# Strassen's seven products for the down projection of a two-layer decoder trunk

## The chip, the cores and the metric

The kernel runs on one core of one Trainium2 chip. The metric is the device time of one launch in microseconds. The core has TensorE (PE: matmuls; PEld: its weight loads), VectorE (DVE), ScalarE (ACT), GpSimd (POOL) and SyncE (SP, which issues DMAs here). Each takes its instructions in order and waits on semaphores for the others.

## The reference

Two layers of a hybrid decoder block over 256 tokens of 1024 features, all in float32. The first half of a layer (attention, a recurrent branch, a pooling branch, gates, an output projection) is not touched. The second half is the MLP:

```python
m = rms_norm(h, norm_mlp_pre[l])
y = jnp.square(jax.nn.relu(m @ w_mlp_up[l])) @ w_mlp_down[l]
h = h + rms_norm(y, norm_mlp_post[l])
```

Here m is 256 x 1024, w_mlp_up is 1024 x 4096 and w_mlp_down is 4096 x 1024.

## The kernel before

**Precision.** Each float32 operand is split into a high part, rounded to the fast format fp32r by ACT (`A.activation(hi, src, AF.Copy)`, L84), and a low part, the rest, by DVE (`V.tensor_tensor(... op=ALU.subtract)`, L85). A product is then three matmuls into the same PSUM bank: high by high, high by low, low by high (`mm3`, L91 to L94). So every weight that is used passes once through ACT and once through DVE.

**Weights.** They lie in memory as tiles of 128 x 1024 in the order of use. `load_to` (L130) issues a DMA on SP into one of four raw buffers (`NRAW`); `split_to` (L138) makes the pair `wh`, `wl` in one of eight buffers each; `take` hands out the next pairs in order, and `ahead` (L159) splits two tiles in advance. A raw buffer is free again when its last reader is done, and the DMA of a later tile waits for that.

**The MLP.** The 4096 hidden features are done in eight chunks of 512. `up` (L725) makes one chunk: for each of its two units of 256 features `w_unit` (L276) issues 48 matmuls of 256 columns into one bank, ACT takes the ReLU and the square, and the result is split into `hid`. The first chunk (`up_first`, L698) is made with tokens as rows and is turned by PE transposes (`hidden_T`). `down` (L737) adds one chunk's part of the result into four PSUM banks `yb` (two halves of tokens by two halves of output columns) that stay open over all chunks: for each 256 hidden features 24 matmuls of 512 columns (`s_hu`, L289). The order on PE is up of chunk f, then down of chunk f - 1. The last two chunks are done token half by token half, so that the norm of the first half (`residual`, L253) runs beside the matmuls of the second.

**What sets the order.** A scheduler in the tile framework puts each engine's instructions in order from the program's order, priorities and its own estimate of durations, and gives each new tile of a pool the buffer that it expects to be free first. The order is fixed when the program is built.

Of the kernel before, what the change touches and what calls it, by code (L numbers as in the profile page):

```python
# [16 lines left out]
L = 2  # L17
D = 1024
# [14 lines left out]
AHEAD = 2  # L33
RGD = 4
FINE = (8, 8)
SQRT_2_PI = 0.7978845608028654


# [13 lines left out]

def trunk(ctx, tc, x, wts, rgw, par, gpost, eye, ctab, out):
    nc = tc.nc
    V, A, PE = nc.vector, nc.scalar, nc.tensor

    const = ctx.enter_context(tc.tile_pool(name="const", bufs=1))
    raws = ctx.enter_context(tc.tile_pool(name="raws", bufs=NRAW))
# [14 lines left out]
    def ttile(shape, dt=F32, nm="t"):  # L73
        return tmp.tile(shape, dt, tag="t", name=nm)
# [4 lines left out]
    def bank(shape, nm="ps"):  # L79
        return psum.tile(shape, F32, tag="b", name=nm)  # L80

    def split(hi, lo, src, scale=None):
        if scale is None:
            A.activation(hi, src, AF.Copy)  # L84
            V.tensor_tensor(out=lo, in0=src, in1=hi.bitcast(F32), op=ALU.subtract)  # L85
        else:
            A.activation(hi, src, AF.Copy, scale=scale)
            V.scalar_tensor_tensor(out=lo, in0=src, scalar=scale, in1=hi.bitcast(F32),
                                   op0=ALU.mult, op1=ALU.subtract)
# [244 lines left out]
    for l in range(L):  # L334
# [355 lines left out]

        gB = gpool.tile([P, D], F32, tag="g", name="gB2")
        nc.sync.dma_start(gB[:], gpost[l, 1])
        yb = [[bank([P, 512]) for _ in range(2)] for _ in range(2)]

        def new_hidden():
            return (acts.tile([P, 2, 4, T], F32R, tag="hi", name="hid"))

        def up_first():  # L698
            hus = take(4)
            hid = new_hidden()  # L700
            zs = []

            def hidden_T(tt):
                p2 = bank([P, 4, P])
                for j in range(4):
                    PE.transpose(p2[:, j, :], zs[tt][:, j * P:(j + 1) * P], ident)
                split(hid[:, 0, :, tt * P:(tt + 1) * P], hid[:, 1, :, tt * P:(tt + 1) * P], p2[:])

            for tt in range(2):
                ps = bank([P, 512])  # L710
                for u in range(2):
                    w = [[t_.rearrange("p (k n) -> p k n", k=4)[:, k, :] for hu in hus[2 * u:2 * u + 2]
                          for k in range(4) for t_ in hu[i:i + 1]] for i in range(2)]
                    by_pass(ps[:, u * 256:(u + 1) * 256], uh, ul, w[0], w[1], tt,
                            mid=(lambda: mlp_in(1)) if tt == 0 and u == 1 else None)
                z = ttile([P, 512], nm="z")
                A.activation(z[:], ps[:], AF.Relu)
                V.tensor_tensor(out=z[:], in0=z[:], in1=z[:], op=ALU.mult)
                zs.append(z)
            later(1, lambda: hidden_T(0))  # L720
            later(1, lambda: hidden_T(1))
            ahead()
            return hid

        def up(fc):  # L725
            hid = new_hidden()
            for u in range(2):
                ps = w_unit(take(2), uh, ul)
                tick()
                z = ttile([P, 2, T], nm="z")  # L730
                A.activation(z[:], ps[:], AF.Relu)
                A.activation(z[:], z[:], AF.Square)
                split(hid[:, 0, 2 * u:2 * u + 2, :], hid[:, 1, 2 * u:2 * u + 2, :], z[:])
                ahead()
            return hid

        def down(fc, hid):  # L737
            for nh in range(2):
                for i in range(2):
                    hu, = take(1)  # L740
                    for tt in range(2):
                        s_hu(yb[tt][nh][:], hu, hid[:, 0], hid[:, 1], 2 * i, tt, fc == 0 and i == 0, False)
                    ahead()

        hid = up_first()
        for fc in range(1, 7):
            nxt = up(fc)
            down(fc - 1, hid)
            hid = nxt
        hids = [hid, up(7)]  # L750
        hus = take(8)
        un = []
        if l + 1 < L:
            uh, ul = new_pair("u")
        for tt in range(2):
            for f in range(2):
                for nh in range(2):
                    for i in range(2):
                        if tt == 1 and f == 1 and nh == 1 and i == 0 and l + 1 < L:
                            mix_features(0, un[0], l + 1)  # L760
                        s_hu(yb[tt][nh][:], hus[4 * f + 2 * nh + i], hids[f][:, 0], hids[f][:, 1], 2 * i, tt,
                             False, f == 1 and i == 1)
            residual(tt, yb[tt], msq[tt], gB)
            if l + 1 < L:
                un.append(mix_norm(tt))
            else:
                for hf in range(2):
                    sl = slice(hf * 512, (hf + 1) * 512)
                    nc.sync.dma_start(out[tt * P:(tt + 1) * P, sl], h[:, tt, sl])
# [37 lines left out]
def _layout(i):  # L807
    qc = np.concatenate([np.arange(hd * 64, hd * 64 + 64) for hd in _HEADS])
    units, rg, par, gp = [], [], [], []
    for l in range(L):  # L810
        w = i["w_in"][l]
        o = np.cumsum([0, 1024, 256, 256, 1024, 1024, 1024, 1024, 1024, 1024])
        q, kv, xr, yr, pp = w[:, :1024][:, qc], w[:, 1024:1536], w[:, o[3]:o[4]], w[:, o[4]:o[5]], w[:, o[5]:o[6]]
        ga, gr, gpl = w[:, o[6]:o[7]], w[:, o[7]:o[8]], w[:, o[8]:o[9]]
        units.append(_s_units(kv)[0])
        for u in _s_units(q):
            units.append(u)
        by = {"pg": i["w_pool_groups"][l].reshape(2, 2, 2, P, 256).transpose(0, 3, 1, 2, 4).reshape(2, 1, P, HU_COLS)}
        for nm, m in (("pp", pp), ("yr", yr), ("xr", xr)):
            by[nm] = _w_units(m).reshape(4, 2, P, HU_COLS)  # L820
        for nm, m in (("gp", gpl), ("ga", ga), ("gr", gr), ("bp", i["w_pool_br"][l]), ("ba", i["w_attn_br"][l][qc]),
                      ("br", i["w_rnn_br"][l])):
            by[nm] = _s_units(m)
        for nm in ORDER:
            units.append(by[nm[0:2]][int(nm[2])])
        for u in _s_units(i["w_out"][l]):
            units.append(u)
        up = _w_units(i["w_mlp_up"][l]).reshape(8, 4, P, HU_COLS)
        dn = _s_units(i["w_mlp_down"][l]).reshape(2, 8, 2, P, HU_COLS).transpose(1, 0, 2, 3, 4).reshape(8, 4, P, HU_COLS)
        units.append(up[0])  # L830
        for f in range(1, 8):
            units.append(up[f])
            units.append(dn[f - 1])
        units.append(dn[7])
# [34 lines left out]
```

## Time and profile before

| | us |
|---|---|
| median of 2 runs (964.25 to 965.38) | 964.82 |
| the profiled execution | 964.16 |
| its span, first to last instruction | 962.3 |
| down projection of layer 0, first matmul | 326.4 |
| last matmul of the program | 955.55 |

The granted TensorE clock is 0.999 of full speed. The rows that carry the argument stand in the prediction. To read them: a row of a timeline is start, duration, engine, line, operation, output<-inputs; the bracket is the engine's idle time just ahead and what ended it. A row of a group has the count, the busy time, the mean in ns, then the idle time before.

### The profile page before, as it was taken

Reading aid. Unit: us, or ns where it says so; the run is one execution under the profiler, and the core shown is the slowest. Engines: PE = TensorE matmul, PEld = TensorE weight load, DVE = VectorE, ACT = ScalarE, POOL = GpSimd, SP = SyncE. Lnnn points to the kernel's source line nnn. Section 1 sums busy time; section 2 is a strip of 40 time slices with the busy share of each in tenths; the row PEclk is TensorE's granted clock in tenths of the full one; section 3 lists DMA queues with packets and bytes.
Section 4 is the critical chain, followed back from the end, with each engine's and each line's share of the span. In section 5 each row is a group of like instructions: output and inputs, shape, how many; then the busy total and the mean of one; then the engine's idle time right before and its main releaser. Section 6 shows DMA issues by size and latency. Waiting matters only on the chain.

```text
span 962.3 us, 14953 instructions
## 1 busy us (share of the span) xinstructions
PE 951.3 (99%) x5716; PEld 835.3 (87%) x5716; DVE 649.7 (68%) x1101; ACT 599.8 (62%) x1001; POOL 2.6 (0%) x20
## 2 busy tenths in 40 slices
PE   8999999999999999999999999999999999999997
PEld 5898988988888999999888989888888899999995
DVE  6877886779768645445586778777897585545542
ACT  7754864789737655455566657566895476555541
POOL 0000000000000000000000000000000000000000
PEclk9999999999999999999999999999999999999999
DMA  7765456453755766665457536536358285665631
GB/s 277 244 205 185 132 166 195 161 178 111 254 161 176 226 192 192 183 192 176 134 183 257 172 111 210 179 103 219 124 178 262 88 276 179 195 185 188 185 122 44
DMA packets 48743, 173.28 MB, mean 180 GB/s; under 512 B 5408, under 2 KB 5792, under 8 KB 48672
## 3 DMA queue, kind: packets, MB, share of 16 engines
q1 hardware_dynamic: 48384, 172.16, 55.4%
q8 instruction: 45, 0.74, 0.3%
q14 instruction: 26, 0.21, 0.1%
q10 hardware_dynamic: 288, 0.17, 0.1%
HBM read 171.26 MB, written 1.05 MB: 179 GB/s over the span
## 4 chain that ended last, share of the span: by engine, by line
PE 97%; DMA 1%; ACT 1%; DVE 1%; issue 0%; SPq 0%; DVEq 0%; ACTq 0%
PE ps L92 28%; PE ps L93 28%; PE ps L94 28%; PE ps L303 8%; PE ps L391 1%; PE ps L439 1%; PE ps L428 1%; DMA raw<-wts 1%; PE ps L216 1%; PE ps L371 0%; PE ps L619 0%; ACT wh L84 0%; DVE h L269 0%; ACT junk L229 0%; DVE wl L85 0%
## 5 line engine op out<-in xcount | busy, mean ns | idle before, releaser
L85 DVE TENSOR_TENSOR wl<-raw,wh 128x1024 fp32r<-128x1024 f32 (+1 forms) x348 | 385.7, 1123 | 189.1 <-ACT wh L84 180.4
L84 ACT ACTIVATE wh<-raw 128x1024 fp32r<-128x1024 f32 (+1 forms) x348 | 334.2, 986 | 242.6 <-PE ps L94 106.2
L92 PE MATMUL ps<-mh,wh 128*128 128x256 f32 x448 | 126.9, 283 | 0.0
L94 PE MATMUL ps<-mh,wl 128*128 128x256 f32 x448 | 126.8, 283 | 0.0
L93 PE MATMUL ps<-ml,wh 128*128 128x256 f32 x448 | 126.8, 283 | 0.0
L92 PE MATMUL ps<-uh,wh 128*128 128x256 f32 x384 | 109.0, 284 | 0.0
L93 PE MATMUL ps<-ul,wh 128*128 128x256 f32 x384 | 108.7, 283 | 0.0
L94 PE MATMUL ps<-uh,wl 128*128 128x256 f32 x384 | 108.6, 283 | 0.0
L93 PE MATMUL ps<-wl,hid 128*128 128x512 f32 x256 | 99.9, 390 | 0.0
L92 PE MATMUL ps<-wh,hid 128*128 128x512 f32 x256 | 99.8, 390 | 0.0
L94 PE MATMUL ps<-wh,hid 128*128 128x512 f32 x256 | 99.6, 389 | 0.0
L92 PEld LDWEIGHTS ps<-mh,wh 128*128 128x128 f32 x448 | 86.0, 192 | 0.5
L93 PEld LDWEIGHTS ps<-ml,wh 128*128 128x128 f32 x448 | 85.9, 192 | 0.5
L94 PEld LDWEIGHTS ps<-mh,wl 128*128 128x128 f32 x448 | 86.0, 192 | 0.0
L92 PE MATMUL ps<-wh,uh 128*128 128x512 f32 x200 | 79.2, 396 | 0.7 <-ACT uh L222 0.7
L94 PE MATMUL ps<-wh,ul 128*128 128x512 f32 x200 | 78.1, 390 | 0.4 <-DVE ul L224 0.4
L93 PE MATMUL ps<-wl,uh 128*128 128x512 f32 x200 | 78.1, 390 | 0.0
L92 PEld LDWEIGHTS ps<-uh,wh 128*128 128x128 f32 x384 | 73.6, 192 | 1.1 <-issue 0.7
L93 PEld LDWEIGHTS ps<-ul,wh 128*128 128x128 f32 x384 | 73.6, 192 | 0.4
L94 PEld LDWEIGHTS ps<-uh,wl 128*128 128x128 f32 x384 | 73.6, 192 | 0.0
L94 PEld LDWEIGHTS ps<-wh,hid 128*128 128x128 f32 x256 | 48.1, 188 | 10.0
L92 PEld LDWEIGHTS ps<-wh,hid 128*128 128x128 f32 x256 | 48.1, 188 | 9.7
(190 smaller groups left out, 1589.8 us busy)
## 6 DMA issues: line engine op xcount, KB each, us to landing
raw<-wts SPq DMA_DIRECT2D x316, 512.0 KB, 4.3
gB<-gpost SPq DMA_DIRECT2D x4, 512.0 KB, 4.6
rg<-rgw SPq DMA_DIRECT2D x8, 256.0 KB, 3.9
out<-h SPq DMA_DIRECT2D x4, 256.0 KB, 2.1
h<-x SPq DMA_DIRECT2D x2, 256.0 KB, 3.3
h<-x SPq DMA_DIRECT2D x1, 512.0 KB, 7.0
cst<-ctab SPq DMA_DIRECT2D x1, 168.0 KB, 4.8
prm<-par ACTq DMA_DIRECT2D x1, 104.0 KB, 3.7
```

Of the source, the lines that this page charges most:

```text
L84: A.activation(hi, src, AF.Copy)
L85: V.tensor_tensor(out=lo, in0=src, in1=hi.bitcast(F32), op=ALU.subtract)
L92: PE.matmul(o, lh, rh, start=start, stop=False, **kw)
L93: PE.matmul(o, lh, rl, start=False, stop=False, **kw)
L94: PE.matmul(o, ll, rh, start=False, stop=stop, **kw)
L216: PE.transpose(banks[c // 4][:, c % 4, :], src[c // 4][:, (c % 4) * P:(c % 4 + 1) * P], ident)
L303: PE.matmul(o, xx[:, c, tsl], ww[c], start=(n == 0 and c == 0), stop=(n == 2 and c == 7))
L391: PE.matmul(sc[hd // hp][:, hd % hp, :], qT[a, j // 2][rows, j % 2, blk * P:(blk + 1) * P], kTs[0][rows, a, 0:w], start=True, stop=True)
L428: PE.transpose(ps[:, g, :], g8["p"](4 * b + g)[:, kt * P:(kt + 1) * P], ident)
L439: PE.matmul(ps[b * 64:b * 64 + 64, :, :], vt[kt][:, 256 + kv * 64:256 + kv * 64 + 64], g8[b, kt][:], start=(kt == 0), stop=(kt == nk - 1))
```

## The change

The down projection is done in 16 blocks (`NBLK`) of 256 hidden features. In the first 13 of layer 0 and 14 of layer 1 a block's product, 256 tokens by 256 features times 256 features by 1024 columns, is taken as a 2 x 2 block product and computed by Strassen's scheme in Winograd's form: seven products of 128 x 128 by 128 x 512, each of three matmuls, in place of eight. Each product adds into a bank of its own over all these blocks (`prods`, seven banks), and five additions at the end (`drain`) combine them. The last three and two blocks (`PLAIN`) are done as before, into the same banks.

The scheme needs four sums of weight quarters (`weight_sums`) and four of activation quarters (`hidden_forms`) per block. They are computed on POOL. Of the operands, b11 of the second weight tile (`bh`, `bl`), the first weight tile (`dh`, `dl`) and the four weight sums (`sh`, `sl`, two pairs) are split, and so are three quarters and four sums of the activations (`xf`). The host puts the weight tiles in another order and swaps the halves of every second tile of a block.

```diff
+PLAIN = (3, 2)
+NBLK = 16
...
+            for j in range(2):
+                zs[j] = ttile([P, 2, T], nm="z")
...
-                split(hid[:, 0, :, tt * P:(tt + 1) * P], hid[:, 1, :, tt * P:(tt + 1) * P], p2[:])
+                for j in range(2):
+                    A.activation(zs[j][:, :, tt * P:(tt + 1) * P], p2[:, 2 * j:2 * j + 2, :], AF.Copy)
...
+        def up(j):
+            ps = w_unit(take(2), uh, ul)
+            tick()
+            z = ttile([P, 2, T], nm="z")
+            A.activation(z[:], ps[:], AF.Relu)
+            A.activation(z[:], z[:], AF.Square)
+            zs[j] = z
+        def hidden_forms(j):
+            z = zs.pop(j)
+            a12, a22, a11, a21 = [z[:, i // 2, (i % 2) * P:(i % 2 + 1) * P] for i in range(4)]
+            sm = ttile([P, 4, P], nm="sm")
+            G.tensor_tensor(sm[:, 0, :], a21, a22, op=ALU.add)
+            G.tensor_tensor(sm[:, 2, :], a11, a21, op=ALU.subtract)
+            G.tensor_tensor(sm[:, 1, :], sm[:, 0, :], a11, op=ALU.subtract)
+            G.tensor_tensor(sm[:, 3, :], a12, sm[:, 1, :], op=ALU.subtract)
+            f = acts.tile([P, 2, 7, P], F32R, tag="hi", name="xf")
+            zf = z.rearrange("p c t -> p (c t)")[:, 0:384]
+            split(f[:, 0, 0:3, :].rearrange("p b t -> p (b t)"), f[:, 1, 0:3, :].rearrange("p b t -> p (b t)"), zf)
+            split(f[:, 0, 3:7, :], f[:, 1, 3:7, :], sm[:])
+            forms[j] = f
+        def weight_sums(j):
+            load_to(st["split"] + 2)
+            r0, r1 = raw_t.pop(st["split"]), raw_t.pop(st["split"] + 1)
...
+            b21, b22, b12, b11 = r0[:, 0:512], r0[:, 512:1024], r1[:, 0:512], r1[:, 512:1024]
+            t8 = acts.tile([P, 4, 512], F32, tag="lo", name="wsum")
+            G.tensor_tensor(t8[:, 0, :], b22, b12, op=ALU.subtract)
+            G.tensor_tensor(t8[:, 1, :], b12, b11, op=ALU.subtract)
+            G.tensor_tensor(t8[:, 2, :], b22, t8[:, 1, :], op=ALU.subtract)
+            G.tensor_tensor(t8[:, 3, :], b21, t8[:, 2, :], op=ALU.subtract)
...
+            split(w1[0][:], w1[1][:], r0[:])
+            split(w4[0][:], w4[1][:], b11)
+            wforms[j] = [w1, w4, t8]
+            load_to(st["split"] + 3)
+        def weight_forms(j):
+            t8 = wforms[j].pop()
+            for i in range(2):
...
+                split(w[0][:], w[1][:], t8[:, 2 * i:2 * i + 2, :].rearrange("p b n -> p (b n)"))
+                wforms[j].append(w)
+        def down(j):
+            f = forms.pop(j)
+            w1, w4, w2, w3 = wforms.pop(j)
+            lo_, up_ = slice(0, 512), slice(512, 1024)
+            for p, blk, w, cs in ((2, 0, w1, lo_), (1, 2, w4, lo_), (3, 6, w1, up_), (5, 3, w2, up_), (7, 5, w2, lo_),
+                                  (6, 4, w3, lo_), (4, 1, w3, up_)):
+                if p not in prods:
+                    prods[p] = bank([P, 512], nm="pr")
+                first, last = j == 0, j == nstr - 1 and p in (1, 5, 6, 7)
+                mm3(prods[p][:], f[:, 0, blk, :], f[:, 1, blk, :], w[0][:, cs], w[1][:, cs], first, last)
+        up_first()
+        split_to(st["use"] + 2)
+        up(2)
+        weight_sums(0)
+        split_to(st["use"] + 2)
+        weight_forms(0)
+        hidden_forms(0)
+        for j in range(nstr):
+            if j + 3 < NBLK:
+                up(j + 3)
+            if j + 1 < nstr:
+                weight_sums(j + 1)
+                hidden_forms(j + 1)
+            if j + 4 < NBLK:
+                split_to(st["use"] + 2)
+            down(j)
+            if j + 1 < nstr:
+                weight_forms(j + 1)
...
+            s1 = ttile([P, 512], nm="s1")
+            A.activation(s1[:], prods[1][:], AF.Copy)
+            u2, u4, u3 = [ttile([P, 512], nm="us") for _ in range(3)]
+            V.tensor_tensor(out=u2[:], in0=prods[6][:], in1=s1[:], op=ALU.add)
+            V.tensor_tensor(out=u4[:], in0=prods[5][:], in1=u2[:], op=ALU.add)
+            V.tensor_tensor(out=u3[:], in0=prods[7][:], in1=u2[:], op=ALU.add)
+            u5 = ttile([P, 512], nm="us")
+            V.tensor_tensor(out=u5[:], in0=prods[7][:], in1=u4[:], op=ALU.add)
+            return [[s1, u4], [u3, u5]]
...
+            for nh in range(2):
+                V.tensor_tensor(out=ys[nh][:], in0=tgt[tt][nh][:], in1=ys[nh][:], op=ALU.add)
+            residual(tt, ys, msq[tt], gB)
```

**How the order moves.** On PE an up projection of 48 matmuls and a block's 21 of the down projection now alternate. Three other places matter, all in the middle of layer 0's MLP.

ACT before, one chunk: `z` is the hidden chunk, `wh` the high parts of weight tiles (the number behind the name is the tile's place in memory).

```order
314 L731 ACTIVATE z_3866<-ps_3817 128x512
315 L732 ACTIVATE z_3866<-z_3866 128x512
316 L84 ACTIVATE hid_3816<-z_3866 128x512
317 L84 ACTIVATE wh124_4076<-raw124_3983 128x1024
318 L84 ACTIVATE wh125_4080<-raw125_4001 128x1024
319 L731 ACTIVATE z_3932<-ps_3883 128x512
320 L732 ACTIVATE z_3932<-z_3932 128x512
321 L84 ACTIVATE hid_3816<-z_3932 128x512
```

ACT now, a little over one block: `wh126`, `wh127` are up weights; `dh_4042`, `bh_4044`, `sh_4097`, `sh_4101` belong to the block with raw tiles 120 and 121, whose weight sums are `wsum_4037` and whose activations are `xf_4059`.

```order
333 L87 ACTIVATE sh_4097<-wsum_4037 128x1024
334 L87 ACTIVATE sh_4101<-wsum_4037 128x1024
335 L732 ACTIVATE z_4034<-ps_3985 128x512
336 L87 ACTIVATE bh_4044<-raw121_3952 128x512
337 L733 ACTIVATE z_4034<-z_4034 128x512
338 L87 ACTIVATE dh_4162<-raw124_4052 128x1024
339 L87 ACTIVATE xf_4059<-sm_4054 128x512
340 L87 ACTIVATE wh126_4184<-raw126_4074 128x1024
341 L87 ACTIVATE xf_4179<-z_3914 128x384
342 L87 ACTIVATE wh127_4188<-raw127_4170 128x1024
343 L87 ACTIVATE sh_4217<-wsum_4157 128x1024
344 L87 ACTIVATE sh_4221<-wsum_4157 128x1024
```

Ahead of the split of an up tile stands now the form of `sm` (row 339), which waits for POOL. Before, only PE and the loads were waited for there.

POOL had 8 memsets a layer and nothing in the MLP. Its rows now, with the semaphores that they wait for (DMAHW are the loads): the sums of raw tiles 124 and 125, then the activation sums of the block ahead of them, then the sums of raw tiles 128 and 129.

```order
59 L759 TENSOR_TENSOR wsum_4157<-raw124_4052,raw125_4072 128x512 [waits DMAHW1_49,DMAHW0_49,DVE_49]
60 L760 TENSOR_TENSOR wsum_4157<-raw125_4072 128x512
61 L761 TENSOR_TENSOR wsum_4157<-raw124_4052,wsum_4157 128x512 [waits Pool_49]
62 L762 TENSOR_TENSOR wsum_4157<-raw124_4052,wsum_4157 128x512 [waits Pool_49]
63 L742 TENSOR_TENSOR sm_4054<-z_3794 128x128
64 L743 TENSOR_TENSOR sm_4054<-z_3794 128x128
65 L744 TENSOR_TENSOR sm_4054<-sm_4054,z_3794 128x128 [waits Pool_49]
66 L745 TENSOR_TENSOR sm_4054<-z_3794,sm_4054 128x128 [waits Pool_49]
67 L759 TENSOR_TENSOR wsum_4277<-raw128_4172,raw129_4192 128x512 [waits DMAHW5_49,DMAHW4_49,DVE_49]
```

So `sm_4054`, of the block with raw tiles 120 and 121, is made only after the weight sums of the next block (rows 59 to 62), and those wait for that block's raw tiles.

SP, the loads, before and then now, with their waits: tiles in the order in which they are used.

```order
134 L134 DMA raw123_3965<-wts 128x1024 [waits DMAHW3_49,DVE_49]
135 L134 DMA raw124_3983<-wts 128x1024 [waits DMAHW4_49,DVE_49]
136 L134 DMA raw125_4001<-wts 128x1024 [waits DMAHW5_49,DVE_49]
137 L134 DMA raw126_4019<-wts 128x1024 [waits DMAHW6_49,DVE_49]
138 L134 DMA raw127_4084<-wts 128x1024 [waits DMAHW7_49,DVE_49]
```

```order
135 L137 DMA raw124_4052<-wts 128x1024 [waits DMAHW4_49,DVE_49,Pool_49]
136 L137 DMA raw125_4072<-wts 128x1024 [waits DMAHW6_49,DVE_49]
137 L137 DMA raw126_4074<-wts 128x1024 [waits DMAHW7_49,DVE_49]
138 L137 DMA raw127_4170<-wts 128x1024 [waits DMAHW5_49,DVE_49]
139 L137 DMA raw128_4172<-wts 128x1024 [waits DMAHW0_49,DVE_49,Pool_49]
140 L137 DMA raw129_4192<-wts 128x1024 [waits DMAHW2_49,DVE_49]
```

Before, each load waits for the DVE split of the tile that held its buffer. Now the first raw tile of every block waits for POOL (128 takes the buffer of 124, after its last sum), and the second takes the buffer of an up tile: 129 that of 126, so that it waits for the DVE half of the split of `wh126`.

More of the change, by code (lines that the diff above doesn't have):

```diff
@@ L54, in trunk @@
     nc = tc.nc
-    V, A, PE = nc.vector, nc.scalar, nc.tensor
+    V, A, PE, G = nc.vector, nc.scalar, nc.tensor, nc.gpsimd
     const = ctx.enter_context(tc.tile_pool(name="const", bufs=1))
@@ L692, in trunk @@
         nc.sync.dma_start(gB[:], gpost[l, 1])
-        yb = [[bank([P, 512]) for _ in range(2)] for _ in range(2)]
-        def new_hidden():
-            return (acts.tile([P, 2, 4, T], F32R, tag="hi", name="hid"))
+        nstr = NBLK - PLAIN[l]
+        prods = {}
+        zs, forms, wforms = {}, {}, {}
         def up_first():
             hus = take(4)
-            hid = new_hidden()
-            zs = []
+            toks = []
+            for j in range(2):
+                zs[j] = ttile([P, 2, T], nm="z")
             def hidden_T(tt):
@@ L705, in hidden_T @@
                 for j in range(4):
-                    PE.transpose(p2[:, j, :], zs[tt][:, j * P:(j + 1) * P], ident)
-                split(hid[:, 0, :, tt * P:(tt + 1) * P], hid[:, 1, :, tt * P:(tt + 1) * P], p2[:])
+                    PE.transpose(p2[:, j, :], toks[tt][:, j * P:(j + 1) * P], ident)
+                for j in range(2):
+                    A.activation(zs[j][:, :, tt * P:(tt + 1) * P], p2[:, 2 * j:2 * j + 2, :], AF.Copy)
             for tt in range(2):
@@ L715, in up_first @@
                             mid=(lambda: mlp_in(1)) if tt == 0 and u == 1 else None)
-                z = ttile([P, 512], nm="z")
+                z = ttile([P, 512], nm="zt")
                 A.activation(z[:], ps[:], AF.Relu)
                 V.tensor_tensor(out=z[:], in0=z[:], in1=z[:], op=ALU.mult)
-                zs.append(z)
+                toks.append(z)
             later(1, lambda: hidden_T(0))
             later(1, lambda: hidden_T(1))
[L722 to L751, printed above, removed]
+        def up(j):
[5 more added lines that the diff above has]
+            zs[j] = z
@@ new lines, in weight_sums @@
+        def weight_sums(j):
+            load_to(st["split"] + 2)
+            r0, r1 = raw_t.pop(st["split"]), raw_t.pop(st["split"] + 1)
+            st["split"] += 2
+            st["use"] += 2
+            b21, b22, b12, b11 = r0[:, 0:512], r0[:, 512:1024], r1[:, 0:512], r1[:, 512:1024]
[4 more added lines that the diff above has]
+            G.tensor_tensor(t8[:, 3, :], b21, t8[:, 2, :], op=ALU.subtract)
+            w1 = (his.tile([P, HU_COLS], F32R, tag="wh", name="dh"), los.tile([P, HU_COLS], F32R, tag="wl", name="dl"))
+            w4 = (ttile([P, 512], F32R, nm="bh"), ttile([P, 512], F32R, nm="bl"))
+            split(w1[0][:], w1[1][:], r0[:])
+            split(w4[0][:], w4[1][:], b11)
+            wforms[j] = [w1, w4, t8]
+            load_to(st["split"] + 3)
@@ new lines, in weight_forms @@
+        def weight_forms(j):
+            t8 = wforms[j].pop()
+            for i in range(2):
+                w = (his.tile([P, HU_COLS], F32R, tag="wh", name="sh"), los.tile([P, HU_COLS], F32R, tag="wl", name="sl"))
+                split(w[0][:], w[1][:], t8[:, 2 * i:2 * i + 2, :].rearrange("p b n -> p (b n)"))
[10 more added lines that the diff above has]
+                mm3(prods[p][:], f[:, 0, blk, :], f[:, 1, blk, :], w[0][:, cs], w[1][:, cs], first, last)
@@ L752, in trunk @@
+        hids = []
+        for j in range(nstr, NBLK):
+            hid = acts.tile([P, 2, 2, T], F32R, tag="hi", name="hid")
+            z = zs.pop(j)
+            split(hid[:, 0], hid[:, 1], z[:])
+            hids.append(hid)
+        hus = take(2 * PLAIN[l])
         un = []
@@ L754, in trunk, with drain @@
             uh, ul = new_pair("u")
-        for tt in range(2):
[L756 to L763, printed above, removed]
+        def drain():
+            s1 = ttile([P, 512], nm="s1")
[7 more added lines that the diff above has]
+            return [[s1, u4], [u3, u5]]
+        rest = drain()
+        full = bank([P, 512], nm="pr")
+        tgt = [[prods[2], prods[3]], [prods[4], full]]
+        for tt in range(2):
+            for nh in range(2):
+                for b, hid in enumerate(hids):
+                    if tt == 1 and nh == 1 and b == PLAIN[l] - 1 and l + 1 < L:
+                        mix_features(0, un[0], l + 1)
+                    for k in range(2):
+                        wh, wl = hus[2 * b + k]
+                        cs = slice(nh * 512, (nh + 1) * 512)
+                        xs = [hid[:, i, k, tt * P:(tt + 1) * P] for i in range(2)]
+                        mm3(tgt[tt][nh][:], xs[0], xs[1], wh[:, cs], wl[:, cs],
+                            tt == 1 and nh == 1 and b == 0 and k == 0, b == PLAIN[l] - 1 and k == 1)
+            ys = [rest[tt][nh] for nh in range(2)]
+            for nh in range(2):
+                V.tensor_tensor(out=ys[nh][:], in0=tgt[tt][nh][:], in1=ys[nh][:], op=ALU.add)
+            residual(tt, ys, msq[tt], gB)
             if l + 1 < L:
@@ L827, in _layout @@
             units.append(u)
[L828 to L834, printed above, removed]
+        up = _w_units(i["w_mlp_up"][l]).reshape(NBLK, 2, P, HU_COLS)
+        dn = i["w_mlp_down"][l].reshape(NBLK, 2, P, D)
+        nstr = NBLK - PLAIN[l]
+        pairs = [np.stack([d[0], np.concatenate([d[1][:, 512:], d[1][:, :512]], 1)]) for d in dn]
+        units += [up[0], up[1], up[2], pairs[0], up[3]]
+        for j in range(nstr):
+            if j + 1 < nstr:
+                units.append(pairs[j + 1])
+            if j + 4 < NBLK:
+                units.append(up[j + 4])
+        units += [dn[j] for j in range(nstr, NBLK)]
         blk = np.zeros((4, P, 2, 2, P), np.float32)
```

## The prediction

> **What bounds the kernel now.** I read the page's first parts, then the PE timeline, the windows by stage, and then the rows of the engines that feed PE.
>
> ```profile
> span 962.3 us, 14953 instructions
> PE 951.3 (99%) x5716; PEld 835.3 (87%) x5716; DVE 649.7 (68%) x1101; ACT 599.8 (62%) x1001; POOL 2.6 (0%) x20
> ...
> PE 97%; DMA 1%; ACT 1%; DVE 1%; issue 0%; SPq 0%; DVEq 0%; ACTq 0%
> ```
>
> PE is busy for 99% of the span and is 97% of the chain that ended last: every matmul taken out shortens the run, as long as its operands come no later. What a matmul costs is read from start to start, since "busy" overlaps:
>
> ```profile
> 394.63 0.39 PE L93 MATMUL ps<-wl,hid 128*128 128x512 f32 x1
> ...
> 404.38 0.39 PE L94 MATMUL ps<-wh,hid 128*128 128x512 f32 x1
> 404.60 0.28 PE L92 MATMUL ps<-mh,wh 128*128 128x256 f32 x1
> ...
> 410.84 0.28 PE L93 MATMUL ps<-ml,wh 128*128 128x256 f32 x1
> ```
>
> From 394.63 to 404.60 there are 44 matmuls of 512 columns: 9.97/44 = 0.2266 us each. From 404.60 to 410.84 there are 52 of 256 columns: 0.120 us each. The profiled row for one block (256 hidden features) is 48 up matmuls, 48 x 0.120 = 5.76 us, and 24 down matmuls, 24 x 0.2266 = 5.44 us: 11.20 us. In the MLP stretch PE has no gap, and DVE and ACT have half of the time free:
>
> ```profile
> core 0: us, PE busy (x) PEld busy (x) DVE busy (x) ACT busy (x) POOL busy (x), PEclk, DMA share, GB/s
> ...
> 380.00:430.00 50.00, 50.00 (x324) 45.82 (x323) 24.83 (x22) 25.73 (x30) 0.00 (x0) 1.00 0.63 190
> ```
>
> **What the change removes.** A Strassen block has 7 products of 3 matmuls in place of 24 matmuls: 3 fewer. With 13 such blocks in layer 0 and 14 in layer 1, 27 x 3 = 81 matmuls go (the built programs hold 5628 and 5547): 81 x 0.2266 = 18.4 us. PE's own work per block becomes 5.76 + 21 x 0.2266 = 10.52 us. That it does what it says is thus settled; the question is whether the operands come every 10.52 us.
>
> **What it adds on ACT and DVE.** Durations of a split, and the hop between the engines:
>
> ```profile
> 409.00 1.06 ACT L84 ACTIVATE wh<-raw 128x1024 fp32r<-128x1024 f32 x1 [3.13 <-PE ps L93]
> ...
> 411.40 0.58 ACT L731 ACTIVATE z<-ps 128x512 f32<-128x512 f32 x1
> ...
> 412.67 0.63 ACT L84 ACTIVATE hid<-z 128x512 fp32r<-128x512 f32 x1
> ...
> 410.09 1.22 DVE L85 TENSOR_TENSOR wl<-raw,wh 128x1024 fp32r<-128x1024 f32 x1 [2.96 <-ACT wh L84]
> ...
> 413.34 0.69 DVE L85 TENSOR_TENSOR hid<-z,hid 128x512 fp32r<-128x512 f32 x1 [0.58 <-ACT hid L84]
> ```
>
> DVE starts 0.03 us after ACT's 1.06 us end. Per block ACT now has five 1024-column halves of a split (5 x 1.06), the ReLU (0.58), the square, bh and the 512-column form (0.63 each), and a 384-column form (about 0.52, between): 8.3 us. DVE has 5 x 1.22 + 2 x 0.69 + 0.55 = 8.0 us. Both stay under 10.52, so neither is the bound by its sum. With seven product banks held, one bank is left for the up projection, so the next up waits for the ReLU before it; by ACT's order that ReLU ends about 6.0 us after the form of sm begins, and the up then ends with its first two products 1.5 us before the next form is there, so this is hidden while the loop below is as long as I make it.
>
> **What it adds on POOL, and the loop it closes.** Two orders meet. POOL's rows (shown with the change) put the four weight sums W of block k+1 ahead of the four hidden sums S of block k. ACT's rows put the form of sm of block k, which waits for S, ahead of the split of the next up weights (wh126 in those rows), and the second raw tile of a down pair (raw129) gets the buffer that this up tile (raw126) held. So from one form of sm to the next runs one closed chain, each block:
>
> ACT form of sm, ACT wh, DVE wl, load of the raw tile, POOL 4 W (128x512), POOL 4 S (128x128), the next form of sm.
>
> PE's third product of every block reads that form, so the period is the longer of this loop and 10.52. Before, a load waits for a split too, but with no sum of POOL between the load and the next split:
>
> ```profile
> SPq L134 <- DVE wl L85: 728.0, 288, 14.2
> ...
> DMA to landing us min/median/max: 3.4/4.1/5.5
> ```
>
> The second line is of the raw loads between 400 and 440 us, which overlap one another. In the loop the load stands nearly alone (its partner left some 5 us earlier): I take 3.7, with ends 3.4 and 4.1.
>
> POOL's price is the unknown; before, POOL only has memsets, so it is bounded by these and by DVE:
>
> ```profile
> L488 POOL MEMSET xp<- 128x32 f32 x8 | 1.0, 125 | 425.6 <-ACT junk L229 280.0 <-DVE sw L496 56.9 <-DVE qkv L347 42.7
> ...
> L861 POOL MEMSET const-float32-1.0<- 128x1 f32 x1 | 0.1, 99 | 0.0
> ...
> L347 DVE TENSOR_TENSOR qkv<-rt,rt 128x128 f32<-128x128 f32 x8 | 2.3, 287 | 0.1
> ```
>
> 31 more elements cost 26 ns: 0.84 ns for each in one stream, 0.10 us fixed. A sum has three streams, two read and one written. One after the other they make 0.10 + 3 x 0.84 x 0.512 = 1.39 us for 128x512 and 0.42 for 128x128: the upper end. DVE's price for the same shapes, 0.69 and 0.29, is the lower end. I take 1.2 and 0.4, nearer the upper one, as that is from POOL's own rows: 4 x 1.2 + 4 x 0.4 = 6.4 us (ends 3.9 and 7.2). The Trainium skill (GPSIMD Engine Reference, Elementwise — side-by-side cycle accounting) gives 4497 ns for such an add of 2048 columns; by its quarter and sixteenth, 1.12 and 0.28, POOL's part would be an estimated 5.6 us and the total below 994; no run shows it yet.
>
> The loop: 0.63 + 0.03 + 1.06 + 0.03 + 1.22 = 2.97 (ACT and DVE), 0.25 for the hops to SP, POOL and back (estimate, the seen one being 0.03), 3.7 (load), 6.4 (POOL): 13.3 us. That is 2.8 us over PE's 10.52. It turns once for every form of sm that has weight sums ahead of it and a form before it: blocks 1 to 11 in layer 0, 1 to 12 in layer 1, 23 turns: 23 x 2.8 = 64.4 us.
>
> **Start and end of the MLP.** The first two blocks reach PE by transposes; before, these begin at 319.8 and the down projection at 326.4:
>
> ```profile
> L706 PE MATMUL ps<-idt,z x16: 271/272/273, 319.8 to 793.2; 128*128 128x128 f32 x16
> ...
> L92 PE MATMUL ps<-wh,hid x256: 388/389/396, 326.4 to 954.7; 128*128 128x512 f32 x128
> ```
>
> The new path behind them (about 1.1 of transposes, four half-size copies, 1.7, S, 1.6, form, 1.35) ends near 325.6, two products ahead of need, if POOL has done W of block 1 by then, which hangs on loads at the busiest place. I take 1 us a layer (ends 0 and 4). The five adds after the last product lie beside 10.9 us or more of plain matmuls. At the end
>
> ```profile
> 955.31 0.24 PE ps L94
> 955.55 0.02 issue
> 955.57 0.79 ACT junk L229 x2
> ```
>
> the sum of squares starts right after the last matmul; now a DVE add of 0.69 (as hid's) stands between, and nothing covers it: 0.7 us.
>
> **The sum.** The profiled execution took 964.16 us (1.9 around its span of 962.3; the median of the runs is 964.82). 964.2 - 18.4 + 64.4 + 2 + 0.7 = 1012.9, so 1013 us.
>
> **Rivals.**
>
> 1. POOL adds at DVE's price. Loop 2.97 + 0.25 + 3.7 + 3.9 = 10.8, 0.3 over PE: 23 x 0.3 = 7, total 964.2 - 18.4 + 7 + 2.7 = 956: the gain shows, not slower. It decides where the four W and four S together fall under 4.3 us, for then the loop is under the 11.2 of before. For it: 0.84 ns per element is no slower than DVE's stream. Against: that is a stream with nothing to read. Chance 0.15.
>
> 2. POOL and DVE exclude one another. If an addition on POOL cannot read while DVE runs an instruction with two operands in SBUF, the whole DVE instruction in front is waited for. When the raw tile lands, 6.8 us into the loop, DVE still has the end of a sum's split, bl and dl before it, until 9.1 by the durations above: 2.3 us more, loop 15.6, 23 x 5.1 = 117, total 1066. The trace has no POOL read, so nothing speaks for it or against it. The Trainium skill (SBUF — State Buffer, Who interferes with whom) states just this: a VectorE instruction with two SBUF inputs contends with a GpSimd instruction that reads SBUF, and the second to issue is blocked until the first ends; by that rule the change would be this rival. Chance 0.22.
>
> 3. Nothing in the loop is late (the load finds its buffer sooner than the order tells). Then all of the 18.4 comes less 2.7: 948.5. The order of the program speaks against it. Chance 0.03.
>
> The forecast itself has 0.60. Its own range is from a POOL part of 5.1 (two of the three streams count) with a load of 3.4, loop 11.7, 964.2 + 27 - 15.7 = 976, to 7.2 with 4.1, loop 14.6, 964.2 + 94 - 15.7 = 1042.
>
> **How the numbers follow.** Two per cent, which is about what a measurement of this kernel can tell from no change, is 945.5 and 984.1 around the median. No case reaches 945.5: 0.02 for what I have not seen. Within 2% lie rivals 1 and 3 and the bottom of the forecast's range: 0.20. Slower: 0.78. The range leaves out rivals 1 and 3 and reaches from just under the forecast's own low end to just over rival 2: 974 to 1068.
>
> **What would show it.** Right: PE has a gap of 2 to 4 us in each block, ended by the form of sm (ACT or DVE), at full granted clock; POOL's 128x512 takes near 1.2 us and its four sums follow the landing of a raw tile at once; loads on SP wait for wl and for POOL; POOL is busy for about half of the MLP. Wrong: PE without gaps in the MLP (rivals 1 and 3); POOL's additions that stretch while DVE runs, or DVE's that grow over 1.22 (rival 2); gaps ended by the ReLU or by sl, which would put another chain in the loop's place; or a granted clock that falls because PE now pauses, which I price at nothing since it stays 1.00 in every stretch before.

## The result and the profile after

The changed kernel takes 1061.22 us (median of 2 runs, 1060.84 to 1061.61) against 964.82 before: 1.0999 times as long, interval 1.0978 to 1.102. It is slower by 96 us, where the prediction had 48.

The first view is the page of the changed kernel (engines, chain), then its waits (what, in total, how often, the longest) and its window of the MLP of layer 0.

```profile
PE 978.1 (92%) x5635; PEld 834.0 (79%) x5635; DVE 762.1 (72%) x1194; ACT 640.6 (60%) x1088; POOL 227.7 (21%) x236
...
PE 56%; POOL 20%; DMA 10%; DVE 5%; ACT 5%; issue 3%; SPq 0%; ACTq 0%; POOLq 0%; DVEq 0%
...
ACT xf L87 <- POOL sm L745: 182.9, 25, 8.2
POOL wsum L759 <- DMA raw<-wts: 134.9, 21, 9.3
...
PE pr L95 <- ACT xf L87: 57.0, 23, 3.2
...
380.00:430.00 50.00, 41.78 (x251) 35.80 (x250) 32.87 (x27) 23.61 (x33) 28.49 (x27) 0.93 0.45 142
```

PE's share of the chain that ended last fell from 97% to 56%, and POOL, the loads, DVE and ACT have most of the rest: with PE the members of the predicted loop. Their waits for one another stand in the two rows in front: the form of sm waits for POOL's last sum, POOL's first sum waits for a load, 25 and 21 times. PE waits 23 times for the form of sm, once for each turn that the prediction counted. In the window no engine is full: POOL 28.5 of 50, DVE 32.9, ACT 23.6, PE 41.8. That is the picture of a closed chain in which the engines wait in turn.

Here is one turn of it, the chain of waits between two forms of sm (start, duration, what):

```profile
404.58 0.04 ACT xf L87
...
405.12 1.05 ACT wh L87
406.19 1.24 DVE wl L88
407.44 3.50 DMA raw<-wts
...
411.10 1.36 POOL wsum L759
412.46 1.71 POOL wsum L760
...
414.24 2.16 POOL wsum L761
...
416.47 1.29 POOL wsum L762
417.76 0.41 POOL sm L742
418.17 0.41 POOL sm L743
418.59 0.42 POOL sm L744
...
419.07 0.47 POOL sm L745
...
419.56 0.04 ACT xf L87
```

It is the loop of the prediction, member by member, and takes 419.56 - 404.58 = 14.98 us: 2.85 on ACT and DVE to 407.43 (forecast 2.97), 3.50 for the load (3.7), 0.17 of hops around it and 0.02 at the end (0.25), and 419.54 - 411.10 = 8.44 on POOL (6.4). All that is over lies in POOL's part, and most of it in the second and third sum: 1.71 and 2.16 us for the same 128x512 that takes 1.29 in the fourth.

The forms of sm of both layers, first and last of the loop, give its mean turn (ACT's timeline: start, duration, operation, idle before and what ended it):

```profile
328.51 0.63 ACT L87 ACTIVATE xf<-sm 128x512 fp32r<-128x512 f32 x1 [3.88 <-POOL sm L745]
...
494.67 0.63 ACT L87 ACTIVATE xf<-sm 128x512 fp32r<-128x512 f32 x1 [7.67 <-POOL sm L745]
...
848.38 0.63 ACT L87 ACTIVATE xf<-sm 128x512 fp32r<-128x512 f32 x1 [3.87 <-POOL sm L745]
...
1029.97 0.63 ACT L87 ACTIVATE xf<-sm 128x512 fp32r<-128x512 f32 x1 [7.64 <-POOL sm L745]
```

11 turns in 166.16 and 12 in 181.59 us: 347.75/23 = 15.12 us a turn, where 13.3 was forecast. What DVE does while POOL's sums stretch, in the same turn as above (DVE's timeline):

```profile
411.21 1.79 DVE L88 TENSOR_TENSOR bl<-raw,bh 128x512 fp32r<-128x512 f32 x1
412.93 2.31 DVE L88 TENSOR_TENSOR dl<-raw,dh 128x1024 fp32r<-128x1024 f32 x1
```

The split's `bl` takes 1.79 in place of 0.69 and `dl` 2.31 in place of 1.22. Read as turns: the first sum runs to 412.46; bl, issued at 411.21, ends 0.54 after that; the second sum, ready at 412.46, ends at 414.17, 1.2 after bl; dl ends 1.1 after the second sum; the third sum 1.2 after dl. Each of the two engines seems to wait until the instruction of the other is over. That is rival 2, and the experiments test it.

### The profile page after: what moved, and what is told of

The parts are those of the page before. It is cut to its first block, busy times and chain, and to the rows that moved or that the text cites. A ratio compares the mean times of both kernels' runs of the same rounds, so it can differ in the third digit from the quotient of the medians.

```text
span 1059.8 us, 15290 instructions
## 1 busy us (share of the span) xinstructions
PE 978.1 (92%) x5635; PEld 834.0 (79%) x5635; DVE 762.1 (72%) x1194; ACT 640.6 (60%) x1088; POOL 227.7 (21%) x236
## 4 chain that ended last, share of the span: by engine, by line
PE 56%; POOL 20%; DMA 10%; DVE 5%; ACT 5%; issue 3%; SPq 0%; ACTq 0%; POOLq 0%; DVEq 0%
PE ps L95 15%; PE ps L97 14%; PE ps L96 14%; DMA raw<-wts 10%; PE ps L306 6%; POOL wsum L761 5%; POOL wsum L760 4%; POOL wsum L759 4%; POOL wsum L762 3%; DVE wl L88 3%; ACT wh L87 3%; PE ps L394 1%; PE ps L442 1%; POOL sm L745 1%; PE ps L431 1%
## 5 line engine op out<-in xcount | busy, mean ns | idle before, releaser
L88 DVE TENSOR_TENSOR wl<-raw,wh 128x1024 fp32r<-128x1024 f32 (+1 forms) x290 | 324.3, 1135 | 71.2 <-ACT wh L87 63.4
L87 ACT ACTIVATE wh<-raw 128x1024 fp32r<-128x1024 f32 (+1 forms) x290 | 274.8, 979 | 118.9 <-PE ps L97 55.2
L87 ACT ACTIVATE xf<-sm 128x512 fp32r<-128x512 f32 x27 | 17.0, 628 | 182.9 <-POOL sm L745 182.9
L759 POOL TENSOR_TENSOR wsum<-raw,raw 128x512 f32<-128x512 f32 x27 | 44.3, 1640 | 363.0 <-DMA raw<-wts 134.9
L88 DVE TENSOR_TENSOR xf<-sm,xf 128x512 fp32r<-128x512 f32 x27 | 18.7, 691 | 134.2 <-ACT xf L87 134.2
L95 PE MATMUL pr<-dh,xf 128*128 128x512 f32 x54 | 25.3, 468 | 57.1 <-ACT xf L87 57.0
L88 DVE TENSOR_TENSOR sl<-wsum,sh 128x1024 fp32r<-128x1024 f32 x54 | 65.8, 1258 | 0.3 <-ACT sh L87 0.3
```

The source lines that it names most:

```text
L95: PE.matmul(o, lh, rh, start=start, stop=False, **kw)
L759: G.tensor_tensor(t8[:, 0, :], b22, b12, op=ALU.subtract)
```

## The experiments

Three theories stood against one another. **Loop**: the closed chain sets the turn, and taking turns with DVE only lengthens it. **Shared read**: DVE and POOL exclude one another, so their work adds up, and that sum alone would hold the turn near 15 us. **POOL slow by itself**: no interference, its additions just cost more than 1.2 and 0.4.

**The price by itself** (`port`). A kernel of its own with stretches of eight instructions each: additions on POOL alone, a subtraction on DVE alone, both together, POOL beside a DVE subtraction that has one operand in PSUM, POOL beside ACT, and zeros written by POOL. It computes nothing of the reference.

```diff
+    for i in range(N):
+        o, q = pool_add(g, b, 512), dve_add(g, b, 1024)
+    g = gate([o, q])
+    for i in range(N):
+        o, q = pool_add(g, b, 512), dve_add(g, ps, 512)
```

> The shared read by itself, nothing of the decoder: additions on POOL (128x512, 128x128) and DVE (128x1024, both operands in SBUF), eight of each, alone and side by side, in seven stretches. Taking turns (an addition on POOL and a DVE instruction with two operands in SBUF exclude one another): POOL alone 1.3 us for 128x512 and 0.42 for 128x128, DVE alone 1.2 us; side by side both engines turn at one common period of 2.3 to 2.5 us, the sum of the two; with one DVE operand in PSUM, beside ACT, or with POOL only writing (memset), each keeps its own pace. POOL slow by itself (no sharing): 1.6 to 1.9 us alone and the same in every stretch. Bandwidth shared by element: both stretch a little, a common period of 1.5 to 2.0 us.

The timelines of POOL and of DVE, eight instructions in each row:

```profile
7.25 9.80 POOL L45 TENSOR_TENSOR po<-b,gate 128x512 f32<-128x512 f32 x8 [6.81 <-ACT gate L40]
17.36 3.33 POOL L45 TENSOR_TENSOR po<-b,gate 128x128 f32<-128x128 f32 x8 [0.32 <-ACT gate L40]
30.59 17.64 POOL L45 TENSOR_TENSOR po<-b,gate 128x512 f32<-128x512 f32 x8 [9.89 <-ACT gate L40]
48.85 9.81 POOL L45 TENSOR_TENSOR po<-b,gate 128x512 f32<-128x512 f32 x8 [0.62 <-ACT gate L40]
```

```profile
20.97 9.17 DVE L50 TENSOR_TENSOR do<-b,gate 128x1024 f32<-128x1024 f32 x8 [20.97 <-ACT gate L40]
30.47 16.63 DVE L50 TENSOR_TENSOR do<-b,gate 128x1024 f32<-128x1024 f32 x8 [0.33 <-ACT gate L40]
48.74 4.88 DVE L50 TENSOR_TENSOR do<-ps,gate 128x512 f32<-128x512 f32 x8 [1.63 <-ACT gate L40]
```

Alone, a 128x512 addition on POOL takes 9.80/8 = 1.23 us, a 128x128 one 3.33/8 = 0.42, and a 128x1024 subtraction on DVE 9.17/8 = 1.15. Side by side the pair takes 17.64/8 = 2.21, almost the 2.38 that the two take one after the other, and a little under the 2.3 to 2.5 expected. With one of DVE's operands in PSUM (and half the width), POOL takes 9.81 for its eight as if alone; beside ACT it took 9.84. So the price in the prediction was right, POOL is not slow by itself, and it is DVE's two SBUF operands that exclude it. The Trainium skill (SBUF — State Buffer, Who interferes with whom) says this, and the two stretches of this run agree with it: 2.21 us for the pair, and no loss with a PSUM operand. The last stretch shows nothing of sharing: POOL's zeros ran from 69.07 to 72.85 us, and DVE's subtractions began at 73.22, after them. In the pair, both engines read the same two tiles; whether that matters is read from a later run.

**The sums left out** (`memset_sums`). POOL writes zeros of the same size in place of all eight sums; the rest of the change stays.

```diff
-            G.tensor_tensor(sm[:, 0, :], a21, a22, op=ALU.add)
+            G.memset(sm[:, 0, :], 0.0)
...
-            G.tensor_tensor(t8[:, 0, :], b22, b12, op=ALU.subtract)
+            G.memset(t8[:, 0, :], 0.0)
...
```

> Leaves out the sums: POOL writes zeros where the eight sums of a block went, and reads nothing. All matmuls, splits and loads stay. If the sums on POOL are the whole cost (by the loop or by the shared read): PE is the bound again, 964 - 18 + 2 to 6 for the start and the end, 948 to 954 us. If PE itself became slower (its clock, the one bank left, the order of the products) or ACT and DVE are the bound: above 964.

The run takes 948.39 us, 16 under the 964.41 of the kernel before on the same chip. Its window of the MLP and two of its forms of sm, seven turns apart:

```profile
380.00:430.00 50.00, 50.00 (x323) 45.60 (x323) 37.20 (x40) 36.89 (x49) 13.00 (x44) 1.00 0.62 196
...
362.45 0.62 ACT L87 ACTIVATE xf<-sm 128x512 fp32r<-128x512 f32 x1
...
436.46 0.62 ACT L87 ACTIVATE xf<-sm 128x512 fp32r<-128x512 f32 x1
```

PE is full at full clock, and a turn takes 74.01/7 = 10.57 us (10.52 were worked out). Everything but the sums comes out as priced in total: 964.2 - 18.4 + 2.7 = 948.5. That it agrees to 0.1 is in part luck, as the start was priced with sums in it, which are left out here, and the turns are 0.05 us longer than worked out.

**Six raw buffers** (`raw6`). With two more raw buffers (and three temporary ones fewer) the second raw tile of a pair no longer gets the buffer of the up tile just ahead; the order of the instructions is the same. This opens the loop at the load.

```diff
-NRAW = 4
-NTMP = 28
+NRAW = 6
+NTMP = 25
```

> Six raw buffers in place of four (and 25 temporaries in place of 28), the instructions in the same order; the second raw tile of a down pair then no longer waits for the up tile's split that follows the form of sm, so the loop through the load is open. If the loop alone sets the period of 15.1 us, and taking turns only lengthens POOL's part of it: the period falls to 10.5 to 11.2 us, 955 to 975 us in all. If DVE and POOL have one read between them, so that their work adds (8.0 + 7.0 us a block) whatever the order: the period stays at 13 to 15 us, 1010 to 1060 us.

The run takes 1027.42 us, 34 less than the changed kernel, but 79 more than with the sums left out. Of 50 us POOL is now busy for 42.57 and DVE for 45.27; forms of sm at 384.46 and, six turns on, at 463.38 give 13.15 us a turn. The loop was real, and something else stands right behind it.

**The activation sums a block earlier** (`s_early`), and **both edges open** (`s_early_raw6`). In the first, `sm` of block j + 2 is made where that of block j + 1 was; its form then no longer waits for the weight sums of the next block. The second adds the six buffers.

```diff
+        hidden_sums(1)
...
+            if j + 2 < nstr:
+                hidden_sums(j + 2)
```

> The four activation sums are made one block earlier (a second copy of sm is held); everything stays on GpSimd and no work is left out. So the form of sm of a block no longer stands behind the weight sums of the next block, and the closed chain of each block loses that stretch: by the durations of the changed kernel it would be about 10.4 us if no engine held another up. Theory 'loop' (the chain of dependences sets the period, and taking turns at the memory only lengthens it): period 10.5 to 11.5 us, total 955 to 975 us, TensorE without gaps in most blocks. Theory 'shared read' (VectorE's and GpSimd's work on two operands in SBUF adds up, about 7.3 + 6.6 us net per block, whatever the order): period 13 to 14 us, total 1010 to 1040 us, near the kernel with six raw buffers, and GpSimd and VectorE each stretched until their busy times fill most of the stretch. Theory 'GpSimd slow by itself': 6.6 us per block do not bound a period of 10.5, total 955 to 975 us.

> As the kernel with the earlier activation sums, with six raw buffers in place of four as well (25 temporary buffers in place of 28), so that both edges of the closed chain are open: the load no longer waits for the split just before, and the form of sm no longer waits for the next weight sums. Theory 'loop': nothing is left to hold a block up, period 10.5 us, total 948 to 960 us. Theory 'shared read': the period stays at 13 to 13.9 us, total 1005 to 1030 us, within 1% of the kernel with six raw buffers alone, and of 50 us VectorE and GpSimd are both busy for over 40. If it falls between (970 to 1000 us), the two take turns only for part of their work and the loop had a part of its own in the kernel with six buffers.

They take 1041.51 and 1020.37 us. Of the second: its window, two forms of sm three turns apart, and a stretch of POOL and DVE.

```profile
380.00:430.00 50.00, 42.84 (x272) 37.94 (x271) 47.88 (x32) 27.19 (x39) 46.48 (x32) 1.00 0.47 158
...
437.79 0.63 ACT L87 ACTIVATE xf<-sm 128x512 fp32r<-128x512 f32 x1 [5.76 <-POOL sm L747]
...
476.96 0.63 ACT L87 ACTIVATE xf<-sm 128x512 fp32r<-128x512 f32 x1 [5.76 <-POOL sm L747]
...
403.41 2.16 POOL L767 TENSOR_TENSOR wsum<-raw,wsum 128x512 f32<-128x512 f32 x1
...
408.64 1.44 POOL L745 TENSOR_TENSOR sm<-z 128x128 f32<-128x128 f32 x1
...
408.28 1.48 DVE L88 TENSOR_TENSOR dl<-raw,dh 128x1024 fp32r<-128x1024 f32 x1
```

With both edges open a turn takes 39.17/3 = 13.06 us, as long as with one open, and PE is still held up. POOL and DVE are now both busy nearly all of the time, 46.5 and 47.9 of 50, and much of that is waiting inside an instruction: 1.44 for a sum of 128x128 that takes 0.42 alone. That sum reads z while DVE reads raw and dh, so the two engines need not read the same tile to hold each other up. By the prices alone POOL has 4 x 1.23 + 4 x 0.42 = 6.6 us of work a block, which would not hold a turn of 10.57; so "POOL slow by itself" falls a second time. The run says "shared read", but a little less than the full sum: the expectation had 6.6 + 7.3 = 13.9 where 13.06 came. The pair of the first run was 0.17 under its sum too, and four to eight such pairs a block would make 0.7 to 1.4 (an estimate). That all of the 13.06 is sharing is not shown: in the two turns from 450.82 to 476.96 the chain that ended last still holds one load of 3.50 us, which waits for `bl` (460.76 to 464.26).

The first of the two missed its range by 1.5 us: its turn is 14.3 (forms at 401.40 and, six turns on, 487.31), over the 13 to 14 expected. In the chain that ended last its load of 4.64 us still waits for a split, and that split stands behind DVE's stretched ones (418.37 to 428.22 for `sl`, `sl`, `bl`, `dl` and `wl`), so a chain through the turns of both engines remained. Neither theory alone gives 14.3; by that chain order and exclusion act together.

**The sums on DVE** (`dve_sums`, and timed as `dve_sums_r`). All eight sums on DVE; POOL is idle.

```diff
-            G.tensor_tensor(sm[:, 0, :], a21, a22, op=ALU.add)
+            V.tensor_tensor(sm[:, 0, :], a21, a22, op=ALU.add)
...
-            G.tensor_tensor(t8[:, 0, :], b22, b12, op=ALU.subtract)
+            V.tensor_tensor(t8[:, 0, :], b22, b12, op=ALU.subtract)
...
```

> The same eight sums on DVE in place of POOL (0.69 and 0.29 us each, 3.9 us a block). DVE then has 8.0 + 3.9 = 11.9 us of work in a block, over PE's 10.52: 23 turns x 1.4 = 32, less 18.4, and 5 for start and end: 975 to 990 us. If it is not the price and place of the sums but waiting for them in that order: near 1061.

> The kernel with all sums on VectorE, once more and timed in rounds: GpSimd's part and the taking of turns are gone, VectorE is busy for nearly all of each block (10.65 us against TensorE's 10.52). One look gave 954.8 us beside 964.4. Theory 'shared read' and theory 'loop' both expect 952 to 958 us, 0.6 to 1.3% under the kernel before, since neither chain nor engine then stands over 10.7 us. If the look was an accident, it comes out at 960 to 968.

The first run took 954.8 us; timed again, the median is 952.76, as expected then, 0.989 of the kernel before (interval 0.9862 to 0.9919). The first expectation was a miss, and for a reason worth knowing: it added up DVE's durations. DVE's timeline of the last kernel below shows what is wrong with that (three sums, the third the first one of the next block):

```profile
384.11 0.69 DVE L759 TENSOR_TENSOR wsum<-raw,raw 128x512 f32<-128x512 f32 x1
384.71 0.69 DVE L760 TENSOR_TENSOR wsum<-raw 128x512 f32<-128x512 f32 x1
...
394.68 0.69 DVE L759 TENSOR_TENSOR wsum<-raw,raw 128x512 f32<-128x512 f32 x1
```

The first row lasts 0.69, but the next starts 0.60 later. By starts, DVE's block, which has no gap between these rows, costs 394.68 - 384.11 = 10.57 us and not the 11.9 of the durations (nor the 10.65 of the two later expectations): just what a turn took with the sums left out.

**The sums on DVE with six raw buffers** (`dve_raw6`), the two edits above together.

> All sums on VectorE, with six raw buffers in place of four (25 temporary buffers in place of 28). If what it loses against the kernel whose sums are left out (948.4 us) is a late load at the ends of the layers' MLP, it comes to 949 to 952 us. If VectorE's own 10.65 us per block and its queue at the ends are the loss, it stays at 953 to 957 us.

```profile
380.00:430.00 50.00, 50.00 (x325) 45.73 (x325) 50.00 (x78) 36.65 (x49) 0.00 (x0) 1.00 0.60 205
```

The median is 947.61 us, 0.9825 of before (interval 0.9809 to 0.9842: under two per cent, but clear of the spread of the runs) and better than both branches of its expectation. PE is full at full clock, DVE shows no idle time, a turn is 10.57 us as with the sums left out (forms of sm at 352.53 and, eight turns on, at 437.07). The buffers are all that this edit adds, so they made up the 5 us that `dve_sums_r` lost; which loads came sooner was not traced. DVE's own 10.57 just fits. This is the fastest of the kernels, 17 us under the one before on the same chip (964.2): of the 18.4 us of matmuls nearly all arrive.

## Why the prediction was right and wrong

**The direction and the chain were right.** The removed matmuls and the small costs at the start and end together come to 948.4 in the run without sums, 948.5 by the prediction, with the luck told there. PE waits for the form of sm 23 times, the load and the split cost what they were priced at, and the loop is the one described.

**The step that failed** is the term of POOL in the loop, 6.4 us, and behind it the weight given to rival 2. The prices 1.2 and 0.4 were right (1.23 and 0.42 alone: 6.6), but they were put into the sum as if DVE did not matter. In the loop POOL took 8.4 us, 1.8 over its price alone, of which 1.4 lie in the second and third sum, beside DVE's `bl` and `dl`. So a turn is 15.12 us and not 13.3, and the 23 turns cost 23 x (15.12 - 10.57) = 105 us against the run without sums, in place of 64.4.

**Rival 2 is what happened**: it had 2.3 us of waiting a turn, a loop of 15.6 and 1066 us; measured are 1.8, 15.1 and 1061. That it came so near is partly luck: it had the first sum wait for all that DVE had in front, where the first sum lost 0.1 us and the second and third alternated with DVE's splits. The 1061 lies in the stated range only since that was drawn to just over rival 2; the forecast's own ended at 1042. Rival 2 got 0.22 because "nothing speaks for it or against it" in a trace without a POOL read. But the forecast itself rested on the contrary, that POOL's price beside DVE is its price alone, for which no row spoke either; the only statement at hand was the one of the Trainium skill that rival 2 cites (SBUF — State Buffer, Who interferes with whom), and its conditions (two SBUF operands on DVE, an SBUF read on POOL) are met here. Rival 1 falls by POOL's price of 1.23. Rival 3, that nothing is late, falls by the waits. (The total for a POOL part of 5.6 us is 964.2 + 46 - 15.7 = 994.5, not below 994.)

**What neither the forecast nor rival 2 held** is that the loop was not alone. Rival 2 counted the exclusion once, as a delay at one place of the loop. It is also a throughput limit: the two engines' work added up to 13 us or more a block in all the orders tried. Had the loop been opened, the kernel would still have been slower (1020 to 1042 us).

**The start** was priced at 2 us for both layers. PE's first matmul that reads the form of sm, and the transposes that begin layer 1, first of the changed kernel and then of the one without sums:

```profile
329.20 0.50 PE L95 MATMUL pr<-dh,xf 128*128 128x512 f32 x1
849.06 0.50 PE L95 MATMUL pr<-dh,xf 128*128 128x512 f32 x1
L219 PE MATMUL ps<-idt,un x16: 272/273/327, 527.6 to 538.3; 128*128 128x128 f32 x16
```

```profile
328.59 0.40 PE L95 MATMUL pr<-dh,xf 128*128 128x512 f32 x1
793.58 0.40 PE L95 MATMUL pr<-dh,xf 128*128 128x512 f32 x1
L219 PE MATMUL ps<-idt,un x16: 272/272/329, 474.5 to 485.2; 128*128 128x128 f32 x16
```

In layer 0 that matmul comes 329.20 - 328.59 = 0.6 us later. In layer 1 it is 2.4 later, counted from the transposes: 849.06 - 527.6 = 321.5 against 793.58 - 474.5 = 319.1. Of the 113.2 us between the profiled executions (1061.6 and 948.4) the turns make 104.6 and the starts 3.0. The other 5.6 come after the last turn of each layer and were not traced further.

**The end** was priced at 0.7, and the chain after the last matmul has a DVE addition of 0.70 us there. (`drain` makes a copy and four additions, not five; one more for each of the four banks of the result follows, and the 0.70 is of these.)

**The clock** was priced at nothing. It did fall, to 0.93 in the window, and nothing shows that it cost anything: the chain of a turn has no piece on PE, and PE's slower matmuls lie inside time in which it would have waited (next section but one). The statement that gaps would come "at full granted clock" was wrong, and the clock before was not 1.00 in every stretch either: it was 0.97 from 940 to 962 us, where PE stops at 955.55. The gaps' size of 2 to 4 us was right but no measure of the loss: the waits in PE's row are 57.0/23 = 2.5 us a turn, while the turn is 4.6 longer than PE's own work; slower matmuls after some of the waits and shorter waits for the ReLU take up the rest.

## What to carry to other kernels

Before work is moved to an idle engine, ask what it shares with the busy one: on this chip POOL's additions and DVE's subtractions on SBUF operands took turns, so the "idle" POOL at 0% of the span had only the time that DVE left. Where two engines take turns, count their work as one engine's sum and check that against the bound, ahead of any chain. And price a busy engine by the distance of its starts, not by its durations: by starts the sums fitted on DVE, with two more load buffers, and the change won 1.75%.

## What the hardware showed that was not expected

After some of its waits PE runs slower for a while. In PE's timeline of the changed kernel, one turn and the start of the next:

```profile
405.26 0.50 PE L95 MATMUL pr<-dh,xf 128*128 128x512 f32 x1 [2.27 <-ACT xf L87]
...
407.86 0.63 PE L95 MATMUL pr<-sh,xf 128*128 128x512 f32 x1
408.29 0.63 PE L96 MATMUL pr<-sl,xf 128*128 128x512 f32 x1
...
410.53 0.28 PE L95 MATMUL ps<-mh,wh 128*128 128x256 f32 x1
...
420.24 0.50 PE L95 MATMUL pr<-dh,xf 128*128 128x512 f32 x1 [2.41 <-ACT xf L87]
...
421.30 0.40 PE L95 MATMUL pr<-sh,xf 128*128 128x512 f32 x1
421.54 0.40 PE L96 MATMUL pr<-sl,xf 128*128 128x512 f32 x1
```

After a gap of 2.27 us the matmuls start 0.34 to 0.59 us apart until 409.14, then 0.23 again; the granted clock in the window is 0.93. The 15 matmuls from 405.26 to 410.53 take 5.27 us in place of 15 x 0.2266 = 3.40: 1.9 us in this turn. The Trainium skill (TensorE: Matmul & The Clock Gate, Why this matters for your kernels) asks for no idle gaps over about 3 us; here a slow stretch followed a gap of 2.27. But the length of a gap alone does not decide it: one turn later, after a gap of 2.41, the matmuls are back at 0.24 us apart from 421.30 on, and PE's timeline of the kernel with both edges open has a longer gap in a window whose granted clock is 1.00:

```profile
416.25 0.38 PE L95 MATMUL ps<-mh,wh 128*128 128x256 f32 x1 [3.14 <-ACT z L732]
```

What decides it stays open.

POOL's zeros, which only write, kept one price beside a DVE that was busy for 37 of 50 us. One group of them in the run without sums (count, shortest, median and longest in ns, first and last start):

```profile
L762 POOL MEMSET wsum<- x27: 522/526/535, 279.9 to 901.8; 128x512 f32 x27
```

And what POOL and DVE lose to each other stands in the profile as busy time, not as waiting: DVE's 47.88 of 50 in the kernel with both edges open looks like a full engine, though DVE's block by starts, without the sums, is 10.57 - 4 x 0.60 - 4 x 0.20 = 7.37 us of a turn of 13.06.
